# Conditioning on POOL's software queue, projections first on ACT's queue, the last load of x in halves

## Chip, cores and metric

One core of a Trainium2 chip. The metric is device microseconds of one execution. The kernel before takes 84.53 us (median of six runs, 84.4 to 85.89). Runs come in two states, fast and slow (over 1.5% above the fastest of the same kernel).

## The reference

```python
# x: 32 x 512 x 256, conditioning: 32 x 64, both projections: 64 x 256, all float32
gamma = conditioning @ gamma_proj
beta = conditioning @ beta_proj
return x * (1 + gamma[:, None, :]) + beta[:, None, :]
```

x and the output have 16.78 MB each. Every element gets one multiplication and one addition, so the work is mostly moving bytes.

## The kernel before

x is cut into four slabs of 8 batches; a slab has 128 partitions with 32 rows of 256 floats. Groups of 16 rows are worked on in place, 11 rows on DVE and 5 on POOL, and stored as 2 MB each. The engines' names: PE multiplies matrices, DVE, ACT and POOL work element by element here, and SP, ACT and POOL issue DMAs. In the profile those of SP and ACT are `hardware_dynamic` (hardware DMAs below), that of POOL is `software_dynamic` (the software queue). A DMA is cut into packets, which sixteen DMA engines share: a store of 2 MB is 128 packets of 16 KB in the trace. It has landed when its semaphore, a counter on which other engines wait, has its last increment.

```python
LOADS = {0: [8, 24]}          # slab 0 as loads of 1 MB and 3 MB; the others 4 MB each
GROUP, ON_DVE = 16, 11

nc.scalar.dma_start(out=cond_s, in_=conditioning)                 # L48, ACT's queue
nc.scalar.dma_start(out=gbproj[:, :dim], in_=gamma_proj)          # L50
nc.scalar.dma_start(out=gbproj[:, dim:], in_=beta_proj)           # L51
for s in range(SLABS):                                            # L59, SP's queue
    for n in LOADS.get(s, [ROWS]):
        nc.sync.dma_start(out=xs[:, r:r+n, :], in_=x_v[s, :, r:r+n, :])
# ... identity on POOL, repeated by DVE (rident, L67) ...
nc.tensor.matmul(cond_T_p, lhsT=cond_s, rhs=rident, ...)          # L72, transposed conditioning
nc.vector.tensor_copy(out=cond_T, in_=cond_T_p)                   # L74
for s in range(SLABS):
    nc.tensor.matmul(p_t, lhsT=cond_T[...], rhs=gbproj, ...)      # L79, gamma and beta of a slab
    nc.scalar.activation(...); nc.scalar.copy(...)                # L82, L85: 1+gamma, beta for POOL
for s in range(SLABS):
    for r0 in range(0, ROWS, GROUP):
        nc.vector.scalar_tensor_tensor(...)                       # L100: (gamma + 1) * x
        nc.gpsimd.tensor_tensor(... mult)                         # L102
        nc.vector.tensor_add(...)                                 # L103: + beta
        nc.gpsimd.tensor_tensor(... add)                          # L104
        nc.scalar.dma_start(out=o_v[s, :, r0:r0+GROUP, :], ...)   # L105: 2 MB store
```

## Time and profile before

| | before |
|---|---|
| median of six runs | 84.53 us |
| span of the profiled run | 82.57 us |
| DMA queues' share of 16 engines | 96.6% |
| DVE, POOL busy | 60%, 56% |
| beta projection lands | 14.6 us |
| first work on x (POOL, DVE) | 17.3, 17.5 us |
| last store issued, landed | 66.7, 81.7 us |

The lines themselves stand in the prediction. The last arithmetic is over at 66.6 us, and 15 us of the span are stores alone.

### The profile page before, as it was taken

How to read it: one execution, taken by the hardware profiler on the slowest of the kernel's cores; microseconds unless marked ns; L12 is line 12 of the kernel's file. 1: busy time of each engine (PE TensorE's matmuls, PEld its weight loads, DVE VectorE, ACT ScalarE, POOL GpSimd, SP SyncE). 2: the span in 40 equal slices, each digit the busy share in tenths (PEclk: the TensorE clock that was granted, in tenths of full speed). 3: DMA queues.
4: the chain of work that ended last, by engine and by line, in shares of the span. 5: the costliest groups of instructions: out<-in, count | busy, mean ns of one | idle time of the engine just before them, and what ended most of it. 6: DMA issues, size and time to landing. Idle time of an engine off the chain costs nothing.

```text
span 82.6 us, 156 instructions
## 1 busy us (share of the span) xinstructions
PE 9.1 (11%) x10; PEld 2.8 (3%) x10; DVE 49.9 (60%) x18; ACT 3.9 (5%) x9; POOL 46.2 (56%) x22
## 2 busy tenths in 40 slices
PE   0080000899600000000000000000000000000000
PEld 0100000443000000000000000000000000000000
DVE  2011000059999999999999999999999920000000
ACT  0600000034400000000000000000000000000000
POOL 2000000069999999999999999999995000000000
DMA  3899999969969989998889979899999999999992
GB/s 56 337 508 397 389 397 524 460 302 508 508 270 492 508 381 381 413 476 381 381 381 556 460 302 460 381 468 421 429 452 389 468 421 421 460 389 452 437 421 87
DMA packets 2080, 33.69 MB, mean 408 GB/s; under 512 B 288, under 2 KB 416, under 8 KB 416
## 3 DMA queue, kind: packets, MB, share of 16 engines
q1 hardware_dynamic: 720, 16.78, 48.6%
q10 hardware_dynamic: 1360, 16.92, 48.0%
HBM read 16.92 MB, written 16.78 MB: 408 GB/s over the span
## 4 chain that ended last, share of the span: by engine, by line
DVE 49%; DMA 16%; issue 11%; PE 2%; ACTq 1%; ACT 1%
DVE xs L100 30%; DVE xs L103 19%; DMA gbproj<-in_beta_proj_dram 16%; PE gb_p L79 2%; ACTq L50 1%; ACTq L48 0%; ACT gb_s L82 0%; ACT gb_s L85 0%
## 5 line engine op out<-in xcount | busy, mean ns | idle before, releaser
L102 POOL TENSOR_TENSOR xs<-xs,gb_s 128x1280 f32<-128x1280 f32 x8 | 23.0, 2895 | 16.2 <-ACT gb_s L82 16.2
L100 DVE SCALAR_TENSOR_TENSOR xs<-gb_p,xs 128x2816 f32<-128x2816 f32 x8 | 24.7, 3083 | 10.9 <-ACT gb_s L85 10.9
L103 DVE TENSOR_TENSOR xs<-xs,gb_p 128x2816 f32<-128x2816 f32 x8 | 24.7, 3086 | 0.3
L104 POOL TENSOR_TENSOR xs<-xs,gb_s 128x1280 f32<-128x1280 f32 x8 | 23.0, 2893 | 0.0
L79 PE MATMUL gb_p<-gbproj,cond_T 64*128 64x512 f32 x8 | 7.2, 1074 | 8.9 <-DMA gbproj<-in_beta_proj_dram 8.9
L74 DVE COPY cond_T<-cond_T_p 64x512 f32<-64x512 f32 x1 | 0.7, 683 | 4.3 <-PE cond_T_p L72 4.3
L79 PEld LDWEIGHTS gb_p<-gbproj,cond_T 64*128 64x128 f32 x8 | 2.5, 328 | 13.7 <-issue 13.7
L72 PE MATMUL cond_T_p<-rident,cond_s 32*64 32x512 f32 x2 | 1.9, 1065 | 3.9 <-DMA cond_s<-in_conditioning_dram 3.9
L82 ACT ACTIVATE gb_s<-gb_p 128x256 f32<-128x256 f32 x4 | 1.5, 383 | 16.4 <-PE gb_p L79 16.4
L85 ACT COPY gb_s<-gb_p 128x256 f32<-128x256 f32 x4 | 1.5, 367 | 0.0
L82 ACT ACT_TABLE_LOAD x1 | 1.3, 1283 | 2.4 <-issue 2.4
L67 DVE COPY rident<-ident 32x512 f32<-32x512 f32 x1 | 0.4, 416 | 1.2 <-POOL ident masks.py:199 1.2
L72 PEld LDWEIGHTS cond_T_p<-rident,cond_s 32*64 32x64 f32 x2 | 0.3, 202 | 3.9 <-issue 3.9
masks.py:197 POOL MEMSET ident<- 32x32 f32 x1 | 0.1, 114 | 0.3 <-POOLq L121 0.3
masks.py:199 POOL TENSOR_SCALAR_AFFINE_SELECT ident<-ident 32x32 f32<-32x32 f32 x1 | 0.2, 202 | 0.1
L121 POOL MEMSET const-float32-0.0<- 128x1 f32 x1 | 0.1, 103 | 0.2 <-issue 0.2
L121 POOL MEMSET const-bfloat16-1.0<- 128x1 bf16 x1 | 0.1, 106 | 0.0
L121 POOL MEMSET const-uint8-127<- 128x1 uint8 x1 | 0.1, 106 | 0.0
L121 POOL MEMSET const-float32-1.0<- 128x1 f32 x1 | 0.1, 103 | 0.0
## 6 DMA issues: line engine op xcount, KB each, us to landing
out_dram<-xs ACTq DMA_DIRECT2D x8, 2048.0 KB, 18.2
xs<-in_x_dram SPq DMA_DIRECT2D x3, 4096.0 KB, 32.9
xs<-in_x_dram SPq DMA_DIRECT2D x1, 3072.0 KB, 12.2
xs<-in_x_dram SPq DMA_DIRECT2D x1, 1024.0 KB, 4.6
gbproj<-in_gamma_proj_dram ACTq DMA_DIRECT2D x1, 64.0 KB, 9.1
gbproj<-in_beta_proj_dram ACTq DMA_DIRECT2D x1, 64.0 KB, 12.9
cond_s<-in_conditioning_dram ACTq DMA_DIRECT2D x1, 8.0 KB, 3.0
```

What stands on the lines that cost most here:

```text
L50: nc.scalar.dma_start(out=gbproj[:, :dim], in_=gamma_proj)
L67: nc.vector.tensor_copy(out=rident.rearrange("p (b g) -> p b g", g=REP), in_=ident.to_broadcast([batch, batch, REP]),)
L72: nc.tensor.matmul(cond_T_p, lhsT=cond_s, rhs=rident, start=True, stop=True)
L74: nc.vector.tensor_copy(out=cond_T, in_=cond_T_p)
L79: nc.tensor.matmul(p_t, lhsT=cond_T[:, s * P : (s + 1) * P], rhs=gbproj, start=True, stop=True)
L82: nc.scalar.activation(out=s_t[:, :dim], in_=p_t[:, :dim], func=mybir.ActivationFunctionType.Identity, bias=1.0, scale=1.0)
L85: nc.scalar.copy(out=s_t[:, dim:], in_=p_t[:, dim:])
L100: nc.vector.scalar_tensor_tensor(out=v, in0=rows(g_p, nv), scalar=1.0, in1=v, op0=ALU.add, op1=ALU.mult)
L102: nc.gpsimd.tensor_tensor(out=w, in0=w, in1=rows(g_s, nw), op=ALU.mult)
L103: nc.vector.tensor_add(out=v, in0=v, in1=rows(b_p, nv))
L104: nc.gpsimd.tensor_tensor(out=w, in0=w, in1=rows(b_s, nw), op=ALU.add)
L121: nc = _bacc.Bacc("TRN2", target_bir_lowering=False, num_devices=1)
```

## The change

The intent is to get gamma and beta sooner. The projections, which land last, become the first DMAs on ACT's queue. The conditioning goes to a queue of its own. The last load of x is halved, so that work on its first half need not wait for its second.

```diff
-    LOADS = {0: [8, 24]}
+    LOADS = {0: [8, 24], 3: [16, 16]}
...
-    nc.scalar.dma_start(out=cond_s, in_=conditioning)
+    nc.gpsimd.dma_start(out=cond_s, in_=conditioning)
     nc.scalar.dma_start(out=gbproj[:, :dim], in_=gamma_proj)
     nc.scalar.dma_start(out=gbproj[:, dim:], in_=beta_proj)
```

## The prediction

> **What bounds the kernel now.** I read the page's row of forty slices first, then the table of stretches for the whole span, and only after that the list of waits and the chain, because the chain alone would mislead here. The slices:
>
> ```profile
> span 82.6 us, 156 instructions
> DMA  3899999969969989998889979899999999999992
> DMA packets 2080, 33.69 MB, mean 408 GB/s; under 512 B 288, under 2 KB 416, under 8 KB 416
> q1 hardware_dynamic: 720, 16.78, 48.6%
> q10 hardware_dynamic: 1360, 16.92, 48.0%
> ```
>
> The reader is to see that the two DMA queues together take 96.6% of the time of all sixteen engines. DVE (60%) and POOL (56%) are far from that, and ACT and PE are nearly idle. The lower digits in the row are packets booked on one side of a slice border; the stretches show that they are no gaps:
>
> ```profile
> 0.00:1.70 1.70, 0.00 (x0) 0.00 (x0) 0.42 (x1) 0.00 (x0) 0.53 (x6) 1.00 0.00 0
> 1.70:81.40 79.70, 9.09 (x10) 2.79 (x10) 49.47 (x17) 3.87 (x9) 45.67 (x16) 1.00 1.00 423
> 81.40:82.60 1.20, 0.00 (x0) 0.00 (x0) 0.00 (x0) 0.00 (x0) 0.00 (x0) 1.00 0.00 0
> ```
>
> The last two columns are DMA share and GB/s. From 1.7 to 81.4 us the engines are busy all the time (1.00), without a hole. So the span is a sum of three terms: 1.7 us until the first packet, 79.7 us of packets, 1.2 us until the last store is confirmed and the program is over. The time reported for that profiled run, 84.35 us, has 1.8 us more outside the span.
>
> Now the waits, which are what the change is aimed at:
>
> ```profile
> POOL xs L102 <- ACT gb_s L82: 16.2, 1, 16.2
> DVE xs L100 <- ACT gb_s L85: 10.9, 1, 10.9
> PE gb_p L79 <- DMA gbproj<-in_beta_proj_dram: 8.9, 1, 8.9
> PE cond_T_p L72 <- DMA cond_s<-in_conditioning_dram: 3.9, 1, 3.9
> ```
>
> and the end of the list of DMA issues:
>
> ```profile
> out_dram<-xs ACTq DMA_DIRECT2D x8, 2048.0 KB, 18.2
> gbproj<-in_gamma_proj_dram ACTq DMA_DIRECT2D x1, 64.0 KB, 9.1
> gbproj<-in_beta_proj_dram ACTq DMA_DIRECT2D x1, 64.0 KB, 12.9
> cond_s<-in_conditioning_dram ACTq DMA_DIRECT2D x1, 8.0 KB, 3.0
> ```
>
> The beta projection is issued at 1.72 us and lands 12.9 us later, at 14.6 us. PE makes gamma and beta from 14.76 us, ACT copies them, and POOL and DVE begin on x at 17.3 and 17.5 us. That wait is real, and the chain that ended last gives it 16% of the span. But that chain ends with the last DVE addition (start 63.49 us, 3.09 us long, so 66.6 us); the last store is issued at 66.7 us and lands 15.1 us later. A store of 2 MB is one eighth of 16.78 MB, and at 429 GB/s or so would take 4.9 us alone. It takes 15.1 us because two older stores stand before it. That queue of about 10 us is the slack of everything that POOL and DVE do.
>
> **Why the projections land so late.** The trace's records of single packets show it. The loads of x move in packets of 8 KB (0.31 us when settled), 24 KB (0.91 us and up) and 32 KB (1.21 us); a row of a projection is a packet of 1 KB and takes 0.05 us. Each of the sixteen engines has four rows of gamma and four of beta, and their starts in the records are 0.95 to 1.0 us apart, with one 24 KB packet of x between any two. So the projections wait for turns, not for bandwidth. The conditioning, two 256 B rows per engine, met the first 1 MB load with its 8 KB packets and was through in 3.0 us.
>
> **What the Trainium skill says.** "DMA: Bandwidth & Descriptors", section "Queues, rings and completion order", says that each engine takes turns between the queue rows that have work, one packet at a time; the 0.95 us spacing above agrees. The same page, section "Issuing engines are not separate DMA queues", says that DMAs from SP, ACT and POOL end on the same 16 engines and interleave. The trace agrees for SP and ACT, since the two queue shares above add up to one full set of engines; for POOL no run shows it yet. The same page's "Latency and other measured facts" gives about 1 us to the first byte for the software path of POOL, against 0.6 us for the hardware path. The kernel before has no such DMA, so this is only the page's figure.
>
> **The change part by part.**
>
> 1. Gamma moves up to the place of the conditioning, issued at 0.74 instead of 1.17 us, and beta to 1.17 instead of 1.72 us. Gamma now needs four turns and one for its semaphore among the 8 KB packets: the conditioning had two and one, and took 3.0 us to land, so two more turns of about 0.35 us make some 3.7 us, landing at 4.5 us instead of 10.3. For beta there are two cases. If its rows are in the ring before gamma's are drained, it keeps its turns and lands at 6 to 8 us; if it falls behind fetched packets of x, as gamma did before (issue 1.17, landing 10.3), it lands at about 10. Estimate: 6 to 10.5, against 14.6.
>
> 2. The conditioning goes through POOL. It leaves later than by ACT and then takes two turns and a semaphore, in the worse case among 24 KB packets (about 1 us each): landing at 4 to 8 us, against 3.7. POOL's identity comes after the issue in POOL's order, maybe 1 us later; the identity is ready at 1.1 us now, so it is no limit. From landing to a ready transposed conditioning is 1.93 us of PE and 0.68 us of DVE (rows of L72 and L74): 7 to 11 us. So the matmuls of gb start between 7 and 11 us instead of 14.76.
>
> 3. POOL and DVE then don't start on x at once: the first group of sixteen rows needs the second load of x, the 3 MB one, which was issued at about 1.2 and needs 12.2 us, so about 13.2 us. Hence the first work on x starts at about 13.3 instead of 17.3 us: 4 us earlier. All stores move up by these 4 us, the first issue from 25.9 to about 22 us, the last from 66.7 to about 62.6.
>
> 4. The fourth load of x is cut into two of 2 MB. Rows per partition become 16 KB packets. A store's 16 KB packet takes 0.611 us, the 32 KB one 1.213: two against one cost 0.009 us more, times eight per engine 0.07 us. The semaphore that the last load waits for becomes that of the 3 MB load instead of gamma's (instruction listing); at 13.2 us two loads of 4 MB are still queued, so SP doesn't starve the engines. The scheduler also puts DVE's first multiplication of slab 3 before the last addition of slab 2, which delays one store by 3.1 us, harmless against a queue of 10 us.
>
> What it makes of the end: the packets are the same 33.69 MB. The first x packet still leaves SP at the same 0.74 us. Sum: 1.7 + 79.7 + 0.07 + 1.2 = 82.7 us span, and 1.8 outside it: 84.5 us. The 4 us that POOL and DVE win turn into 4 us more of waiting for the stores: last store issued at 62.6, landing in about 19 us instead of 15.
>
> **The rivals.** First, that the 4 us go through to the end (80.5 us). The chain and the list of waits speak for it; the 1.00 DMA share in the middle stretch speaks against it, as there is no idle DMA time to take away. I hold it nearly excluded. Second, that earlier stores make the mix of reading and writing slower or faster. The stretches show 419 GB/s for 2 to 26 us (loads), 423 for 26 to 50 (mixed) and 431 for 50 to 81 (stores); moving 4 us from one mix to another at 1 to 2% is below 0.1 us. A slightly slow spell of 32 KB packets lies at 25 to 33 us (1.27 to 1.32 us instead of 1.21), together some 0.5 us; it may move or vanish. Third, that the software queue costs something fixed at the beginning or end of the program or outside the span, which the trace before can't show. One to two us would be 1 to 2.4%. Fourth, that conditioning through POOL comes very late, say 12 us. Then work on x starts at 17 us as before, and the time is unchanged, as the slack of 10 us covers it. Fifth, the two half loads get only half the turns beside stores of equal packets (before, 32 KB against 16 KB gave loads two thirds), so slab 3 lands later: by my count of turns at about 55 us for the second half, when POOL and DVE want it at about 56. A wait of 1 or 2 us there would still be hidden by the stores in the queue.
>
> **Range and chances.** 84.5 us. The three runs before spread from 84.4 to 85.89, so noise alone can move a median by half a us up; down there is only the slow spell of 0.5 us. A fixed cost of the software queue makes the upper side longer. Range 83.9 to 85.6. Faster by over 2% would need 82.9 us, which the sum forbids: 0.02. Slower by over 2%, above 86.3, only by the third rival: 0.06. Within 2%: 0.92.
>
> **What would show it.** Right: the middle stretch has DMA share 1.00 again and about the same length; the beta projection lands before 11 us; DVE and POOL start at about 13.3 us, released by the load of x and not by gamma and beta; DVE ends near 62.5 us; the last store takes about 19 us to land. Wrong: a DMA hole in the middle, a first x packet later than 1.7 us, a tail longer than 1.2 us, or a time outside the span that is more than 1.8 us.

## The result, and the profile after

The changed kernel takes 84.71 us (median of six, 84.53 to 84.95) against 84.53 us. The ratio of the fast runs is 1.0025, 95% interval 1.0003 to 1.0047: the same within 2%, and by the interval a trace slower. Ratios here are the mean time of one kernel's fast runs over that of the other's of the same rounds, so not quite the ratio of the medians quoted.

The head of the page after, with the DMA row and the queues (packets, MB, share of 16 engines):

```profile
span 82.8 us, 158 instructions
DMA  3899999799979988999999999899998999989992
q1 hardware_dynamic: 864, 16.78, 48.7%
q10 hardware_dynamic: 1312, 16.91, 47.8%
q0 software_dynamic: 32, 0.01, 0.0%
```

A third queue has appeared for the conditioning, and the two large shares are as before. The table of stretches for the changed kernel (stretch; its length; busy time of PE, PE's weight loads, DVE, ACT and POOL; clock; DMA share; GB/s):

```profile
0.00:1.70 1.70, 0.00 (x0) 0.00 (x0) 0.00 (x0) 0.00 (x0) 0.66 (x5) 1.00 0.00 0
1.70:81.40 79.70, 9.10 (x10) 2.78 (x10) 49.71 (x18) 3.87 (x9) 46.34 (x19) 1.00 1.00 423
81.40:82.80 1.40, 0.00 (x0) 0.00 (x0) 0.00 (x0) 0.00 (x0) 0.00 (x0) 1.00 0.00 0
```

The engines move bytes at the same 423 GB/s over 79.7 us. The edges of these stretches were set by hand, the same for both kernels; by the packets' own times it is 79.77 us from the first to the last against 79.65 before. Now the list of waits of the changed kernel (engine and line; releaser; us in total, times, longest):

```profile
POOL xs L102 <- ACT gb_s L82: 12.0, 1, 12.0
PE cond_T_p L72 <- DMA cond_s<-in_conditioning_dram: 8.2, 1, 8.2
DVE xs L100 <- ACT gb_s L85: 3.8, 1, 3.8
POOL xs L102 <- DMA xs<-in_x_dram: 1.7, 1, 1.7
PE gb_p L79 <- DMA gbproj<-in_beta_proj_dram: 1.7, 1, 1.7
```

and its DMA issues (queue, count, KB, median us from issue to landing):

```profile
out_dram<-xs ACTq DMA_DIRECT2D x8, 2048.0 KB, 20.6
xs<-in_x_dram SPq DMA_DIRECT2D x2, 2048.0 KB, 41.5
gbproj<-in_gamma_proj_dram ACTq DMA_DIRECT2D x1, 64.0 KB, 5.2
gbproj<-in_beta_proj_dram ACTq DMA_DIRECT2D x1, 64.0 KB, 10.4
cond_s<-in_conditioning_dram POOLq DMA_DIRECT2D x1, 8.0 KB, 6.8
```

The waits at the start did shrink: PE's wait for beta from 8.9 to 1.7 us, DVE's before its first work on x from 10.9 to 3.8. Much of that only moved: PE's wait for the conditioning grew from 3.9 to 8.2 us, so its two waits together went from 12.8 to 9.9. Work on x starts at 14.36 us on POOL and 14.57 on DVE, about 3 us earlier, and ends at 63.4 instead of 66.6 us. But the stores' median from issue to landing grew from 18.2 to 20.6 us. The last one is issued at 63.5 us instead of 66.7 and lands at 81.86 instead of 81.74 us. The 3 us went into the queue of stores.

### The profile page after: what moved, and what is told of

Same layout as the page of the kernel before. It is cut to its first block, busy times and chain, and to the rows that moved or that the text cites. A ratio compares the mean times of both kernels' runs of the same rounds, so it can differ in the third digit from the quotient of the medians.

```text
span 82.8 us, 158 instructions
## 1 busy us (share of the span) xinstructions
PE 9.1 (11%) x10; PEld 2.8 (3%) x10; DVE 49.7 (60%) x18; ACT 3.9 (5%) x9; POOL 47.0 (57%) x23
## 2 busy tenths in 40 slices
DMA packets 2208, 33.69 MB, mean 407 GB/s; under 512 B 272, under 2 KB 416, under 8 KB 416
## 4 chain that ended last, share of the span: by engine, by line
DVE 50%; DMA 13%; issue 9%; PE 2%; ACT 1%; ACTq 1%
DVE xs L100 27%; DVE xs L103 23%; DMA gbproj<-in_beta_proj_dram 13%; PE gb_p L79 2%; ACTq L50 1%; ACT gb_s L82 0%; ACT gb_s L85 0%
## 5 line engine op out<-in xcount | busy, mean ns | idle before, releaser
L48 POOL DMA_DIRECT2D cond_s<-in_conditioning_dram x1 | 0.7, 653 | 0.8 <-POOLq L121 0.8
## 6 DMA issues: line engine op xcount, KB each, us to landing
out_dram<-xs ACTq DMA_DIRECT2D x8, 2048.0 KB, 20.6
gbproj<-in_beta_proj_dram ACTq DMA_DIRECT2D x1, 64.0 KB, 10.4
```

What stands on the lines that cost most here:

```text
L48: nc.gpsimd.dma_start(out=cond_s, in_=conditioning)
```

## The experiments

Three theories stood against each other. **Bandwidth**: the time is the head of 1.7 us, the packets, the tail and 1.8 us outside the span; when the arithmetic happens doesn't matter while the queue of stores is long enough. **Chain**: the end moves as the start of the arithmetic does, as the chain of waits suggests. **Cancelling**: the early start gains something, and the software queue or the halved load takes it back. Each experiment's ratio is to the kernel before in the same rounds.

### The parts one by one

pool_only undoes the halved load:

```diff
-    nc.scalar.dma_start(out=cond_s, in_=conditioning)
+    nc.gpsimd.dma_start(out=cond_s, in_=conditioning)
```

> The kernel before with only the conditioning moved to POOL's queue (gamma and beta thereby first on ACT); the last load of x stays one of 4 MB. Bandwidth theory (time = head of 1.7 us + packets + tail of 1.2 us + 1.8 us outside the span): 84.5 us, ratio to before 0.999 to 1.002; work on x starts at about 14.4 us as in the changed kernel, POOL has no wait of 1.7 us at 56 us. Cancelling theory (the earlier start gives something, the halved last load or the software queue takes it back): if the halved load is what takes it back, this kernel is faster than before by 1 us or more; if the software queue is, it is as slow as the changed kernel, 84.7 us, with a longer tail or a later first packet. Chain theory: 3 us faster, 81.5 us.

Measured: 84.64 us, ratio 1.0013 (0.9998 to 1.0028). Work on x starts at 14.26 us, as in the changed kernel; POOL has no wait for x at 56 us, but it has a longer one for the undivided load, until 51.6 us. From its list of waits:

```profile
POOL xs L102 <- DMA xs<-in_x_dram: 3.1, 1, 3.1
```

So the halved load does shorten POOL's waiting (3.1 to 1.7 us), and that too goes into the queue of stores.

split_only has the halved load and nothing else:

```diff
-    LOADS = {0: [8, 24]}
+    LOADS = {0: [8, 24], 3: [16, 16]}
```

> The kernel before with only the fourth load of x cut into two of 2 MB. Bandwidth theory: +0.07 us of packets at most, 84.6 us, ratio 0.999 to 1.003. Cancelling theory with the halved load as the loss: slower by 1 us or more. Chain theory: nothing, 84.5 us.

Measured: 84.83 us, ratio 1.0044 (1.0025 to 1.0062). This is above the 0.999 to 1.003 expected, a small miss; a tail longer by 0.16 us, explained below, is part of it.

act_order uses neither the software queue nor the halved load:

```diff
-    nc.scalar.dma_start(out=cond_s, in_=conditioning)
     nc.scalar.dma_start(out=gbproj[:, :dim], in_=gamma_proj)
     nc.scalar.dma_start(out=gbproj[:, dim:], in_=beta_proj)
+    nc.scalar.dma_start(out=cond_s, in_=conditioning)
```

> The kernel before with only the order on ACT's queue changed: gamma, beta, conditioning; no software queue, no halved load. Bandwidth theory: 84.5 us, ratio 0.998 to 1.002, though work on x starts at about 14 to 16 us instead of 17.5. Cancelling theory with the software queue as the loss: 81.5 to 83.5 us, as the gain of the order is then left alone. Chain theory: the same.

Measured: ratio of fast runs 1.0025 (1.0003 to 1.0047); two of its seven runs were slow. Its profile fell in the slow state, and in it work on x starts at 19.4 us, not at 14 to 16: the conditioning, behind both projections on one queue, landed 12.0 us after its issue, at about 14 us. So this order isn't an early start in the one trace there is, and it doesn't test what the early start alone gives. pool_only does that better.

What follows: no part is worth 1 us in either direction. The cancelling theory falls, since pool_only has the early start without the halved load and is not faster, and split_only has the halved load without the early start and loses 0.4% (0.6% at the end of its interval, 0.5 us), not the 3 us that would have to be cancelled. That the software queue alone cancels some 3 us is not excluded by these two, and pool_only's 84.64 us with a longer tail is even what that version foretold; the next experiments exclude it from the other side, by delaying and shrinking the arithmetic without any software queue or with the same one.

### Moving the start of the arithmetic

late_1 and late_2 are the kernel before with the projections issued on SP's queue, behind the loads of slabs 0 and 1, or 0, 1 and 2:

```diff
-    nc.scalar.dma_start(out=gbproj[:, :dim], in_=gamma_proj)
-    nc.scalar.dma_start(out=gbproj[:, dim:], in_=beta_proj)
...
         assert r == ROWS
+        if s == 1:                       # 2 in late_2
+            nc.sync.dma_start(out=gbproj[:, :dim], in_=gamma_proj)
+            nc.sync.dma_start(out=gbproj[:, dim:], in_=beta_proj)
```

> The kernel before with the two projections issued on SP's queue behind the loads of slabs 0 and 1, so that they land at about 23 us and work on x starts at about 25.8 instead of 17.5 us, 8.3 us later. Bandwidth theory with a slack of about 10 us in the queue of stores: the last store is issued at about 75 us, when 1.6 us of older packets still stand before it, so 84.5 to 85.5 us. Chain theory: 8.3 us slower, 92.9 us.

Measured: 84.45 us, ratio 0.9994 (0.9969 to 1.002). From late_1's order of time, the first work on x:

```profile
26.11 5.74 POOL L103 TENSOR_TENSOR xs<-xs,gb_s 128x1280 f32<-128x1280 f32 x2 [24.98 <-ACT gb_s L83]
26.32 6.09 DVE L101 SCALAR_TENSOR_TENSOR xs<-gb_p,xs 128x2816 f32<-128x2816 f32 x2 [19.50 <-ACT gb_s L86]
```

and its middle stretch:

```profile
1.70:81.40 79.70, 9.10 (x10) 2.78 (x10) 48.83 (x17) 3.35 (x9) 45.69 (x16) 1.00 1.00 423
```

The arithmetic starts 8.8 us later than in the kernel before, after a wait of 25 us on POOL, and the time doesn't change. In the middle stretch DMA share and GB/s are the same (by the packets' times it is 79.72 us against 79.65). This is the plainest sign of slack: a delay almost three times as long as the change's gain of 3 us costs nothing.

> The same with the projections behind the loads of slabs 0, 1 and 2, landing at about 32.6 us, work on x from about 35.4 us, 17.9 us later than before. Bandwidth theory: the slack of 10 us is used up, the DMA engines run dry between the loads' end and the stores, DVE ends at about 84.5 us and the last store, now alone, takes about 7 us: span about 92.3, time about 94 us, 9.5 us slower and not 17.9. Chain theory: 17.9 us slower, 102.5 us.

Measured: 93.75 us, ratio 1.1098 (1.1066 to 1.1129). The page of late_2:

```profile
span 91.8 us, 155 instructions
DMA  3997999988999969990289005999999899999992
```

and its stretches around the holes:

```profile
41.00:47.00 6.00, 0.00 (x0) 0.00 (x0) 6.00 (x3) 0.00 (x0) 6.00 (x4) 1.00 0.24 104
47.00:90.60 43.60, 0.00 (x0) 0.00 (x0) 36.88 (x13) 0.00 (x0) 34.22 (x12) 1.00 0.87 371
```

Now the slack is used up. The loads end at 41.9 us, the first store is issued at 44.9, and the DMA row shows two holes (slices of 2.3 us with 0 to 2 tenths). Work on x starts 18.2 us later than before, and the time grows by 9.2: the rest, 9 us, was slack. The forecast from the slack was 94 us, the chain's 102.5.

### Less arithmetic, and more bytes

no_adds is the changed kernel without the additions (a wrong result, relative error 0.70):

```diff
-            nc.vector.tensor_add(out=v, in0=v, in1=rows(b_p, nv))
-            nc.gpsimd.tensor_tensor(out=w, in0=w, in1=rows(b_s, nw), op=ALU.add)
```

> The changed kernel without the additions of beta on DVE and POOL (wrong result on purpose): half of the work on x is gone, some 25 us of DVE and 23 us of POOL. Bandwidth theory: the same 33.69 MB, 84.5 us, ratio 0.997 to 1.003. Chain theory: DVE's 18.9% to 23% of the chain fall away, at least 15 us faster, below 70 us.

Measured: 84.84 us, ratio 1.0045 (1.0003 to 1.0088). Its middle stretch:

```profile
1.70:82.30 80.60, 9.10 (x10) 2.79 (x10) 25.54 (x10) 3.87 (x9) 23.54 (x11) 1.00 1.00 418
```

DVE is busy 25.5 instead of 49.7 us and POOL 23.5 instead of 46.3, and nothing is gained. (The profiled run took 85.35 us, the longest of its four, all fast; in the packet records its loads were slow between about 10 and 24 us, by some 1.3 us per engine; see the end.)

extra_load is the changed kernel with 2 MB of x loaded once more:

```diff
+    spare = xpool.tile([P, 16, dim], f32)
+    nc.sync.dma_start(out=spare, in_=x_v[3, :, 16:32, :])
```

> The changed kernel with one more load of 2 MB, the second half of slab 3 once more, into a tile that nobody reads. Bandwidth theory: eight more packets of 16 KB per engine at 0.611 us, 4.9 us: 89.5 us. Chain theory: nobody waits for it, 84.7 us, or little more.

Measured: 89.82 us, ratio 1.0626 (1.0603 to 1.0649). Its middle stretch:

```profile
1.70:86.40 84.70, 9.09 (x10) 2.76 (x10) 49.70 (x18) 3.87 (x9) 46.32 (x19) 1.00 1.00 423
```

A load that nobody waits for costs 5.3 us over the kernel before, 0.3 more than forecast; by the medians it is 5.1 us over the changed kernel. From the first to the last packet it takes 84.70 us against the changed kernel's 79.77, 4.9 us more at the same 423 GB/s; the tail adds 0.2. Half the arithmetic weighs nothing and a useless transfer weighs its full length: the bandwidth theory stands, and the chain theory falls.

### Fewer, larger packets

If only packets count, larger ones should gain a little. big_packets:

```diff
-    LOADS = {0: [8, 24]}
+    LOADS = {}
...
-            nc.scalar.dma_start(out=o_v[s, :, r0 : r0 + GROUP, :],
-                                in_=xs[:, r0 : r0 + GROUP, :])
+        nc.scalar.dma_start(out=o_v[s], in_=xs)      # once per slab
```

> The kernel before with four loads of 4 MB and four stores of 4 MB, so that every packet of x and of the output has 32 KB; the split of the work on DVE and POOL is unchanged. The projections wait for turns of 1.21 us now, so work on x starts later, at about 18 to 19 us, and each store is issued when a whole slab is done. Bandwidth theory: stores take 32 times 1.213 instead of 64 times 0.611 us per engine, 0.3 us less, loads 0.1 to 0.4 us less: 84.1 us, ratio 0.993 to 0.998. Chain theory: work starts 1 to 1.5 us later and the last store is twice as long, so 1 to 6 us slower.

Measured: 84.86 us, ratio 1.0043 (1.0028 to 1.0059), a miss of both theories. In its packet records, the packets do sum up to less: 79.36 us per engine against 79.76 before. Two things ate it. Among 32 KB packets beta landed at 18.5 us, work on x started at 21.2 us, later than the 18 to 19 expected, and the last 4 MB store was issued at 70.6 us, too late to follow on the older one: its first packet left at 71.44 us, when that store's packets were ending (71.2 to 71.7), and at 70.7 to 71.7 us, 13.7 of 16 engines were busy on average. And from the last landing to the end it took 1.14 us instead of 0.83. The second was new, and became a theory: the **tail** depends on where the last store's semaphore stands in the program's closing list of waits. The hardware DMAs take eight semaphores in turn; with 16 of them the last store has the last one. Three more runs test it.

big_stores is the kernel before with only the store's edit above:

> The kernel before with the loads and the first waits as they are and four stores of 4 MB in place of eight of 2 MB. Theory of the packets: 32 packets of 1.213 us instead of 64 of 0.611 us per engine for the stores, 0.29 us less, and no hole this time, since the last store is issued at about 66.9 us and needs 9.7 us of an end at 81. Last packet at 81.1 us. Tail theory (the program's closing list of waits goes on for some 0.04 us per wait behind the last store's): the tail after the landing is longer than before's 0.83 us, by up to 0.3 us, as 12 and not 16 hardware DMAs go round the eight semaphores. Together 84.3 to 84.5 us, ratio 0.997 to 1.000. If packets don't count, 84.5 to 84.8 us.

Measured: 84.52 us, ratio 1.0006 (0.9992 to 1.0021). This is just above the 0.997 to 1.000 expected. There is no hole at 70 us. The tail after the last landing is 1.08 us, as expected, but the last packet ended at 81.5 and not at 81.1 us. The packets do sum to 0.31 us less per engine (79.45 against 79.76). In the packet records the engines finish less evenly: in the last 0.8 us they stand idle for 0.41 us on average, against 0.18 before. So larger packets alone gained nothing.

big_stores_16 adds small cuts that make 16 hardware DMAs of it:

```diff
-    LOADS = {0: [8, 24]}
+    LOADS = {0: [8, 8, 16]}
...
-    nc.scalar.dma_start(out=cond_s, in_=conditioning)
+    nc.scalar.dma_start(out=cond_s[:16], in_=conditioning[:16])
+    nc.scalar.dma_start(out=cond_s[16:], in_=conditioning[16:])
...  (gamma and beta likewise, in halves of 32 rows)
```

> The same four stores of 4 MB, with the three small loads cut into halves by partitions and the 3 MB load into 1 and 2 MB, so that 16 hardware DMAs go round the eight semaphores and the last store has the one that is waited for last, as in the kernel before. Tail theory: 0.83 us from the last landing to the end, span about 82.35 us, time 84.2 to 84.4 us, ratio 0.996 to 0.999: the fastest yet. Without the tail theory: the same as big_stores.

Measured: 84.37 us, ratio 0.9983 (0.997 to 0.9996). The tail after the last landing is 0.83 us again.

cond_halves is the kernel before with only the conditioning cut into two:

```diff
-    nc.scalar.dma_start(out=cond_s, in_=conditioning)
+    nc.scalar.dma_start(out=cond_s[:16], in_=conditioning[:16])
+    nc.scalar.dma_start(out=cond_s[16:], in_=conditioning[16:])
```

> The kernel before with the conditioning's load cut into two of 16 rows, nothing else: 17 hardware DMAs, so that the last store takes another of the eight semaphores. Tail theory: the last packet at 81.4 us as before, the tail after the landing 0.95 to 1.15 instead of 0.83 us, time 84.6 to 84.9 us, ratio 1.001 to 1.004. Without it: 84.5 us, ratio 1.000.

Measured: 84.62 us, ratio 1.0011 (0.9997 to 1.0026), within 1.001 to 1.004, but the interval doesn't exclude 1. Its profile fell in the slow state, so its last packet is late; its tail after the last landing is 0.99 us. All tails, from the last semaphore increment in the trace to the end of the span, are below. No view of the profile lists SP's closing waits, but the instruction records in the kept traces have them. The last two columns come from there: SP's waits that start after the last landing, and the time from the landing until SP is through with them:

| hardware DMAs | kernels | tail, us | waits after | through after, us |
|---|---|---|---|---|
| 16 | before, late_1, late_2, act_order, big_stores_16 | 0.83 to 0.84 | 1 | 0.08 |
| 17 | split_only, cond_halves | 0.99 | 3 | 0.24 |
| 12 | big_stores | 1.08 | 5 | 0.33 |
| 11 | big_packets | 1.14 | 6 | 0.40 |
| 16, one software DMA | changed kernel, no_adds | 0.90 to 0.91 | 1 | 0.08 |
| 15, one software DMA | pool_only | 0.96 | 2 | 0.14 |
| 17, one software DMA | extra_load | 1.12 | 4 | 0.31 |

That the tail goes with the number of DMAs is shown, and these records show how: the number decides which semaphore the last store gets, and so how many waits SP has left once it has landed. Each further wait takes 0.06 us (the theory had 0.04). What follows them, until the end, is 0.74 to 0.75 us in every kernel without a software DMA and 0.81 to 0.82 in those with one; in the changed kernel POOL's clearing of semaphores takes 0.14 us there instead of 0.10. In big_packets the last store's wait is the first of SP's list: it ended 79.2 us of waiting, with five others still to come.

big_stores_16 is faster than the kernel before by 0.17%, with an interval that just excludes 1; its median is 0.34 us below that of the changed kernel, though not of the same rounds. It is the best version found, and it says how little is left: what bounds the kernel is its 33.69 MB. (It also cuts the first loads differently, so not all of the 0.17% need be the tail.)

## Why the prediction was right

**The sum held.** Foretold were 1.7 + 79.7 + 0.07 + 1.2 = 82.7 us of span and 1.8 outside it, 84.5 us; measured were 82.76 of span, 1.77 outside it in the profiled run, and a median of 84.71, inside the range. From the first to the last packet it takes 79.77 us against 79.65 before: of the 0.12 us, some 0.08 is the halved load (its packets of 16 KB took 0.611 us as foretold), the rest is slower packets and not apart from chance. The tail after the last landing is 0.91 instead of 0.83 us, which the sum hadn't: 0.08 us that go with the software queue, in both kernels that have it beside 16 hardware DMAs. These account for the span's 0.19 us. One profile each carries this, and both profiled runs are fast ones for their kernel (84.35 us is below all six runs before, 84.53 the lowest of six after); runs of one kernel spread over 0.4 us.

**The start was off in its parts.** The foretold gamma at 4.5 us was read off the conditioning's 3.0 us; it landed at 5.9, as its first packet came at 4.70 us and not at about 2.2 as the conditioning's had. By then the 8 KB packets were nearly through (the last began at 4.79), so gamma didn't take turns among them, which the prediction had counted on: its four rows per engine went one after the other, in some 0.2 us. Its issue took 0.54 instead of 0.40 us; what the other 2.4 us are isn't settled. Behind it, beta came to lie among the 24 KB packets, with turns of about 1.05 us, and landed at 11.7 us, outside the foretold 6 to 10.5 and after the 11 us that were named as a sign of being right. The conditioning landed at 8.03 us, at the edge of 4 to 8, and its transposed form was ready at 10.8, inside 7 to 11; the matmuls of gamma and beta, foretold for 7 to 11, waited for beta until 11.8.

**One step failed.** "Hence the first work on x starts at about 13.3 instead of 17.3 us" took the second load of x for the releaser. The list of waits shows the releaser as ACT's copies, as before (3.8 us on DVE, 12.0 on POOL); the load had landed at 13.65 us. I had left out that from the first matmul of gamma and beta to the first work on x it takes 2.7 us (14.76 to 17.5 us in the kernel before). The beta projection, then these 2.7 us, set 14.4 us. So 3 us were won there, not 4. As all of it goes into the queue of stores, the size of the gain never touched the time; late_1 shows that even minus 8.8 would not have.

**The late half load** came as the fifth rival had it: it landed at 56.1 us (foretold 55), POOL waited 1.7 us for it, and the stores in the queue covered that.

**Of the rivals,** the first (the gain goes through, 80.5 us) is refuted by the 84.71 us, and late_1 and no_adds show why. The second (another mix of reading and writing) is within the 0.12 us of packets above. The third (a fixed cost of the software queue) is there, but as 0.08 us of tail and not 1 or 2 us; there is none at the head, where the first packet leaves at 1.75 us as before (1.74), nor outside the span. The fourth didn't come: the conditioning landed at 8.03 us, not 12.

## What to carry to other kernels

Before shortening a wait at the start, look for a stretch in which the DMA share is 1.00 from the first packet to the last: here the gain was paid out as a longer queue of stores, and the chain of waits of the kernel before, which ran over DVE, didn't say so. Measure the slack by making the wait worse on purpose; a delay of 8.8 us that costs nothing settles in one run what shaving could not. When only packets are left, count bytes: packet sizes and the DMAs of the program's closing list were worth 0.2% here.

## What the Trainium skill lacked or had wrong

- "DMA: Bandwidth & Descriptors" of the Trainium skill, section "Bandwidth", says without a condition that for transfers between HBM and SBUF the HBM side, about 358 GB/s a core, is the limit. The same section has 425 GB/s measured for loads of 16 MB on a core whose pair is idle. Here a program on one core moved 423 GB/s over 79.7 us, loads and stores mixed: the second figure fits, and the first statement lacks its condition.
- The same page, section "Queues, rings and completion order", rightly says that engines take turns by packet, but lacks what a turn costs beside a stream of large rows: 0.31 us among 8 KB packets, about 1 among 24 KB and 1.21 among 32 KB. So 64 KB of beta took 10.4 us from issue to landing here and 16.8 in big_packets.
- The same page, section "Latency and other measured facts", gives about 1 us to the first byte for the software path and 0.6 us for the hardware path. The first load of x agrees, counted from the end of its issue (1.12 to 1.75 us). The page lacks the time under load: the first packet came 4.7 us after the issue on POOL's queue (1.25 to 5.91 us) and 3.95 us after gamma's on ACT's (0.75 to 4.70), both counted from the start of the issue. Why is open.
- No page has the cost of a program's own closing waits: 0.83 to 1.14 us from the last landing to the end, 0.06 us of it for each further wait that SP has left.
- No page has slow spells of reading. In the two profiles of the slow state (act_order, cond_halves), the loads moved at 389 and 401 GB/s from 5 to 25 us, against 431 in the fast profile before (and 400 in that of no_adds, which counts as fast), at a granted clock of 1.00 throughout; from 35 to 80 us, with the stores under way, they had 425 and 432 against 429. What causes it is open.
